# HGRN2 attention: level operands in places of their own, and the level products of a head in two groups instead of five

## The chip, the cores and the metric

The kernel runs on one core of one Trainium2 chip. The metric is the device time of one execution in microseconds, the median of several executions. A core has a matrix engine (TensorE, PE in the rows, with its weight loads as PEld), a vector engine (VectorE, DVE), a scalar engine (ScalarE, ACT), GpSimd (POOL) and a queue that issues DMAs (SyncE, SP). Each engine takes its instructions in an order that is fixed when the program is built, and they wait for each other through semaphores.

## The reference, cut to what matters

One decoder layer over 2048 tokens of width 1024: an RMS norm, one input projection, an HGRN2 group and a Mamba-2 group side by side, one output projection, a residual and a last norm. The change touches the attention inside a chunk of HGRN2 alone:

```python
q = silu(q_raw);  f = lb + (1 - lb) * sigmoid(f_raw);  k = (1 - lb) * sigmoid(-f_raw)
b = cumsum(log f) over the chunk
att[t, s] = sum over d of q[t, d] * k[s, d] * exp(b[t, d] - b[s, d])      (s <= t)
o = att @ v + (q * exp(b)) @ S;    S = exp(b_last) * S + (k * exp(b_last - b))^T @ v
```

There are 8 heads of 128 x 128. The decay between two tokens differs by channel, so it has to be multiplied into q and k before a matrix product.

## The kernel before, in words

The tokens are taken in four blocks of 512 (`tb` 0 to 3), each as 4 windows of 128. The work of a block is a list of steps: a step is one projection of 128 output columns (24 matmuls of 128x512 in a high and low split, `proj`, line 384), or one of the four steps of `v_step` (line 629). A head of HGRN2 (`hg_unit`) has three of them, `pf`, `pq`, `pg`; a pair of Mamba-2 heads (`m2_unit`) has two, `px`, `pz`. Through most of a block they alternate, H and M, five steps a pair. Each unit brings smaller pieces of work with due steps, counted from its start: after each step `flush` emits those that are due. So the small work of a head stands between the projections of the next units. Inside an engine, a scheduler in the build then sets the order.

For a head, the pieces due at steps 3 to 11 (`DUES`, line 35) are `m0, m1, m2, m3, m4, mk, m5, m6, m7`. The attention of a window is built by levels, each a product of scaled k (as weights) and scaled q (streamed):

- `m0`: the 2x2 pairs on the diagonal, product `A`: 16 matmuls with 32 weight columns and 48 streamed columns (`quarters`, line 692).
- `m1` and `m2`, both `level(b)`, with b of 2 and 8: blocks of b inside groups of 4b, products `B2` and `B8`, 16 matmuls of the same shape each. In each, VectorE first makes the scaled queries in `MB2` or `MB8`, then the products run, then VectorE scales k in place (line 756) for the next level, and picks the wanted entries of the product into `atq` with masks (line 763).
- `m3`: blocks of 32, product `H`, 8 matmuls with 32 weight columns and 32 streamed columns (line 786), after which q and k are scaled in place again (lines 792, 793) and ScalarE copies the result into `att`.
- `m4`: blocks of 64, product `G`, 4 matmuls with 64 weight columns and 64 streamed columns (line 808), then the last scaling in place (lines 814, 815).
- `mk` transposes k (`kT`), `m5` makes the state product `hS` and advances the state, `m6` makes the output `o` from `att` and the states, `m7` collects squares.

Because k and q are scaled where they stand, each level's scaling has to wait for the product of the level before it, which reads the unscaled values. Each fp32 product counts two instructions in the trace, so 16 matmuls show as x32. In the names of the rows, `A`, `B`, `H`, `G` are the banks of these products, `xn`, `S`, `yd`, `yo` those of the Mamba-2 pieces, and `csb`, `xs`, `y`, `ecs` Mamba-2 tiles. Tiles of 512 columns come from one ring of 17 places (`slot("s", ...)`), product banks from one of 6 (`bank`).

Of the kernel before, what the change touches and what calls it, by code (L numbers as in the profile page):

```python
# [7 lines left out]
F32 = mybir.dt.float32  # L8
# [3 lines left out]
ALU = mybir.AluOpType  # L12
# [4 lines left out]
P = 128  # L17
# [17 lines left out]
DUES = (3, 4, 5, 6, 7, 8, 9, 10, 11)  # L35
# [3 lines left out]
def hybrid_layer(ctx, tc, xT, wt, wdt, wout, small, out):  # L39
# [9 lines left out]
    def bank(name):  # L49
        return px.tile([P, TB], F32, tag="mx", name=name)  # L50
# [589 lines left out]
    def hg_unit(tb, hd, ws, vrec, sqs, r):  # L640
# [54 lines left out]
        def m0():
# [25 lines left out]
        def level(b):  # L721
            tot, k, atq = r["tot"], r["k"], r["atq"]
            ng = TB // (4 * b)
            gq = 32 // (4 * b)
            mb = r[f"MB{b}"]
            tt = tot.rearrange("p (g j) -> p g j", j=4)
            tb_ = lambda j, n: tt[:, :, j].unsqueeze(2).broadcast_to([P, ng, n])
            V.tensor_tensor(mb[:, :, 4, :], mb[:, :, 3, :], tb_(2, b), op=ALU.mult)
            V.tensor_tensor(mb[:, :, 5:7, :], mb[:, :, 2:5:2, :],
                            tt[:, :, 1].unsqueeze(2).unsqueeze(3).broadcast_to([P, ng, 2, b]), op=ALU.mult)  # L730
            ps = bank(f"B{b}_{nm}")
            quarters(ps, lambda Q: mb[:, Q * gq:(Q + 1) * gq, 1:7, :].rearrange("p g s r -> p g (s r)"))
            if b == 2:
                r["MB8"] = MB8 = slot("b", [16, 7, 8], f"MB8_{nm}")
                nx = MB8[:, :, 0:4, :].rearrange("p g s (j r) -> p g s j r", r=2)
                src = mb.rearrange("p (g s) j r -> p g s j r", s=4)
                t0 = tot.rearrange("p (g s j) -> p g s j", s=4, j=4)[:, :, :, 0]
                A.copy(nx[:, :, :, 0, :], src[:, :, :, 0, :])
                V.tensor_tensor(nx[:, :, :, 1, :], src[:, :, :, 1, :],
                                t0.unsqueeze(3).broadcast_to([P, 16, 4, 2]), op=ALU.mult)  # L740
                V.tensor_tensor(nx[:, :, :, 2:4, :].rearrange("p g s j r -> p g s (j r)"),
                                src[:, :, :, 5:7, :].rearrange("p g s j r -> p g s (j r)"),
                                t0.unsqueeze(3).broadcast_to([P, 16, 4, 4]), op=ALU.mult)
            else:
                r["qa"] = slot("s", [TB], f"qa{nm}")
                nx = r["qa"].rearrange("p (g j r) -> p g j r", j=4, r=8)
                A.copy(nx[:, :, 0, :], mb[:, :, 0, :])
                V.tensor_tensor(nx[:, :, 1, :], mb[:, :, 1, :], tb_(0, 8), op=ALU.mult)
                V.tensor_tensor(nx[:, :, 2:4, :].rearrange("p g j r -> p g (j r)"),
                                mb[:, :, 5:7, :].rearrange("p g j r -> p g (j r)"), tb_(0, 16), op=ALU.mult)  # L750
            V.tensor_tensor(tt[:, :, 2], tt[:, :, 2], tt[:, :, 3], op=ALU.mult)
            V.tensor_tensor(tt[:, :, 1], tt[:, :, 1], tt[:, :, 2], op=ALU.mult)
            nt = mp.tile([P, ng], F32, tag=f"tot{4 * b}", bufs=1, name=f"tot{4 * b}_{nm}")
            V.tensor_tensor(nt, tt[:, :, 0], tt[:, :, 1], op=ALU.mult)
            kv = k.rearrange("p (g j r) -> p g j r", j=4, r=b)[:, :, 0:3, :]
            V.tensor_tensor(kv, kv, tt[:, :, 1:4].unsqueeze(3).broadcast_to([P, ng, 3, b]), op=ALU.mult)  # L756
            r["tot"] = nt
            av = atq.rearrange("p w (g j r) -> p w g j r", j=4, r=b)
            pv5 = ps[:, 0:192].rearrange("p (w g s r) -> p w g s r", w=NW, s=6, r=b)
# [7 lines left out]

        def m1():
            level(2)

        def m2():
            level(8)
            r["att"] = att = atts[hd % 2]
            for j in range(4):
                qs = slice(32 * j, 32 * j + 32)
                G.tensor_copy(att[qs, :, qs], r["atq"][qs])

        def m3():

            tot, k, qa, att = r["tot"], r["k"], r["qa"], r["att"]  # L780
            ph = bank(f"H{nm}")
            ph2 = ph[:, 0:64].rearrange("p (y c) -> p y c", y=2)
            for w in range(NW):
                for i in range(2):
                    o, p0 = w * P + 64 * i, 64 * (w % 2) + 32 * i
                    T.matmul(ph2[p0:p0 + 32, w // 2, :], lhsT=k[:, o:o + 32], rhs=qa[:, o + 32:o + 64],
                             start=True, stop=True)
            t32 = tot.rearrange("p (g j) -> p g j", j=2)
            q32 = qa.rearrange("p (g j r) -> p g j r", j=2, r=32)
            k32 = k.rearrange("p (g j r) -> p g j r", j=2, r=32)  # L790
            b32 = lambda j: t32[:, :, j].unsqueeze(2).broadcast_to([P, 8, 32])
            V.tensor_tensor(q32[:, :, 1, :], q32[:, :, 1, :], b32(0), op=ALU.mult)
            V.tensor_tensor(k32[:, :, 0, :], k32[:, :, 0, :], b32(1), op=ALU.mult)
            r["t64"] = t64 = mp.tile([P, 8], F32, tag="tot64", bufs=1, name=f"tot64_{nm}")
            V.tensor_tensor(t64, t32[:, :, 0], t32[:, :, 1], op=ALU.mult)
            for a in range(2):
                for i in range(2):
                    A.copy(att[64 * i:64 * i + 32, a::2, 64 * i + 32:64 * i + 64],
                           ph2[64 * a + 32 * i:64 * a + 32 * i + 32, :, :])

        def m4():

            k, qa, att, t64 = r["k"], r["qa"], r["att"], r["t64"]
            ph = bank(f"G{nm}")
            ph2 = ph[:, 0:128].rearrange("p (y c) -> p y c", y=2)
            for w in range(NW):
                o, p0 = w * P, 64 * (w % 2)
                T.matmul(ph2[p0:p0 + 64, w // 2, :], lhsT=k[:, o:o + 64], rhs=qa[:, o + 64:o + 128],
                         start=True, stop=True)
# [50 lines left out]
        def m7():  # L860
# [16 lines left out]
        return [pf_raw, pq_raw, pg_raw] if raw else [pf, pq, pg], list(zip(DUES, (m0, m1, m2, m3, m4, mk, m5, m6, m7)))  # L877
# [336 lines left out]
```

## Time and profile before

| | us |
|---|---|
| median of 3 runs | 1907.94 (1904.02 to 1909.02) |
| the profiled execution, its own time | 1906.3 |
| its span, first to last instruction | 1904.6 |
| PE busy, share of the span | 1871.4 (98%) |
| weight loads busy | 1542.0 (81%) |
| DVE busy | 1183.6 (62%) |
| ACT busy | 707.1 (37%) |
| POOL busy | 295.7 (16%) |

The page gives the busy time of each engine first. The chain that ended last is followed back from the last instruction, and it lists what the end of the program really waited for, in order of time; two pieces of that chain that touch show no gap. A row of a timeline has the start, the time from the first start to the last end, the engine and line, the tiles written and read, and the idle time before it with what ended that.

### The profile page before, as it was taken

Reading aid. Unit: us, or ns where it says so; the run is one execution under the profiler, and the core shown is the slowest. Engines: PE = TensorE matmul, PEld = TensorE weight load, DVE = VectorE, ACT = ScalarE, POOL = GpSimd, SP = SyncE. Lnnn points to the kernel's source line nnn. Section 1 sums busy time; section 2 is a strip of 40 time slices with the busy share of each in tenths; the row PEclk is TensorE's granted clock in tenths of the full one; section 3 lists DMA queues with packets and bytes.
Section 4 is the critical chain, followed back from the end, with each engine's and each line's share of the span. In section 5 each row is a group of like instructions: output and inputs, shape, how many; then the busy total and the mean of one; then the engine's idle time right before and its main releaser. Section 6 shows DMA issues by size and latency. Waiting matters only on the chain.

```text
span 1904.6 us, 33504 instructions
## 1 busy us (share of the span) xinstructions
PE 1871.4 (98%) x13226; PEld 1542.0 (81%) x13226; DVE 1183.6 (62%) x2874; ACT 707.1 (37%) x1175; POOL 295.7 (16%) x390
## 2 busy tenths in 40 slices
PE   7899999999999999999999999999999999999998
PEld 5688887787888888878887887888888877888897
DVE  7678768955575478556664785476456764544452
ACT  4446445533352245234433533343333432211211
POOL 1432242302001211020012111201110130000000
PEclk9999999999999999999999999999999999999998
DMA  7676866754555556455555555554555375424142
GB/s 279 237 267 235 299 253 220 271 177 156 172 187 196 178 178 218 141 173 187 172 199 175 194 193 198 169 189 158 173 186 171 104 239 178 150 83 159 46 143 85
DMA packets 118316, 351.84 MB, mean 185 GB/s; under 512 B 14928, under 2 KB 26352, under 8 KB 117776
## 3 DMA queue, kind: packets, MB, share of 16 engines
q1 hardware_dynamic: 117056, 348.46, 54.4%
q8 instruction: 104, 1.70, 0.4%
q10 hardware_dynamic: 1104, 1.26, 0.2%
q14 instruction: 52, 0.43, 0.1%
HBM read 269.69 MB, written 79.97 MB: 184 GB/s over the span
## 4 chain that ended last, share of the span: by engine, by line
PE 91%; DVE 5%; DMA 2%; issue 1%; ACT 1%; POOL 0%; ACTq 0%; SPq 0%; DVEq 0%; POOLq 0%
PE po L1076 17%; PE px L384 9%; PE pz L384 9%; PE pv L629 9%; PE pf L384 9%; PE pq L384 9%; PE pg L384 8%; PE pB L384 2%; PE pC L384 2%; PE yd L578 2%; PE B L692 2%; PE o L852 1%; PE S L569 1%; PE hS L833 1%; PE yo L589 1%; PE o L851 1%
## 5 line engine op out<-in xcount | busy, mean ns | idle before, releaser
L1076 PE MATMUL po<-mh,woh 128*128 128x512 f32 (+1 forms) x640 | 224.1, 351 | 1.0 <-ACT mh L1064 1.0
L1076 PE MATMUL po<-mh,wol 128*128 128x512 f32 (+1 forms) x640 | 221.9, 347 | 0.2 <-DVE wol L1027 0.2
L1076 PE MATMUL po<-ml,woh 128*128 128x512 f32 (+1 forms) x640 | 220.1, 347 | 0.0
L1076 PEld LDWEIGHTS po<-mh,woh 128*128 128x128 f32 x640 | 121.2, 189 | 19.4 <-ACT mh L1064 2.1
L1076 PEld LDWEIGHTS po<-mh,wol 128*128 128x128 f32 x640 | 121.2, 189 | 15.7 <-issue 0.7
L1076 PEld LDWEIGHTS po<-ml,woh 128*128 128x128 f32 x640 | 120.6, 189 | 15.9 <-DVE ml L1065 0.9
L1064 ACT CAST mh<-mr 128x1024 fp32r<-128x1024 f32 (+1 forms) x41 | 36.1, 883 | 180.7 <-PE po L1076 159.0
L542 DVE TENSOR_SCALAR csb<-csb,cs 128x128 f32<-128x128 f32 x256 | 67.9, 335 | 26.9 <-ACT ecs L539 26.9
L1065 DVE TENSOR_TENSOR ml<-mr,mh 128x1024 fp32r<-128x1024 f32 (+1 forms) x39 | 39.0, 999 | 65.1 <-ACT mh L1064 65.0
L842 DVE SCALAR_TENSOR_TENSOR hSt<-hgS,totw,hS 128x128 f32<-128x128 f32 x32 | 11.0, 345 | 105.8 <-PE hS L833 102.0
L471 DVE SCALAR_TENSOR_TENSOR xs<-u_x,sm,xs 128x512 f32<-128x512 f32 x96 | 71.8, 748 | 4.7 <-ACT xs L469 4.4
L756 DVE TENSOR_TENSOR k<-k,tot 128x384 f32<-128x384 f32 x64 | 43.7, 683 | 47.2 <-PE B L692 47.2
L629 PE MATMUL pv<-wh,hh 128*128 128x512 f32 x224 | 72.0, 403 | 0.0
L468 POOL COPY hist<-u_x 128x3 f32<-128x3 f32 x32 | 9.8, 307 | 399.9 <-ACT u_x L466 399.7
L629 PE MATMUL pv<-wh,hl 128*128 128x512 f32 x224 | 69.3, 391 | 0.0
L629 PE MATMUL pv<-wl,hh 128*128 128x512 f32 x224 | 69.2, 390 | 0.0
L384 PE MATMUL px<-hh,wh 128*128 128x512 f32 x256 | 68.6, 410 | 0.0
L384 PE MATMUL pz<-hh,wh 128*128 128x512 f32 x256 | 67.5, 406 | 0.0
L466 ACT COPY u_x<-px 128x512 f32<-128x512 f32 x32 | 18.7, 585 | 129.9 <-PE px L384 129.9
L601 POOL TENSOR_TENSOR sqa<-sqa,ecs 128x512 f32<-128x512 f32 x24 | 31.6, 1318 | 222.3 <-ACT ecs L600 185.9
L384 PE MATMUL pf<-hh,wh 128*128 128x512 f32 x248 | 65.4, 406 | 0.0
L384 PE MATMUL pg<-hh,wh 128*128 128x512 f32 x248 | 65.3, 404 | 0.0
(339 smaller groups left out, 4565.8 us busy)
## 6 DMA issues: line engine op xcount, KB each, us to landing
wh<-whd SPq DMA_DIRECT2D x156, 512.0 KB, 4.3
wl<-wld SPq DMA_DIRECT2D x156, 512.0 KB, 3.4
whd<-wh SPq DMA_DIRECT2D x52, 512.0 KB, 3.6
wld<-wl SPq DMA_DIRECT2D x52, 512.0 KB, 3.7
wr<-wt SPq DMA_DIRECT2D x51, 512.0 KB, 5.1
csb<-csd SPq DMA_DIRECT2D x32, 512.0 KB, 5.5
mr<-mixd SPq DMA_DIRECT2D x50, 256.0 KB, 2.9
mixd<-sg SPq DMA_DIRECT2D x32, 256.0 KB, 2.1
```

The costliest lines, as they stand in the source:

```text
L384: state["mm"] = T.matmul(ps, lhsT=a[:, k, :], rhs=b[:, k, :], start=(n == 0), stop=(n == 23))
L471: V.scalar_tensor_tensor(dst, u[:, j:j + TB], cw[:, c, j:j + 1], dst, op0=ALU.mult, op1=ALU.add)
L542: V.tensor_scalar(csb[:, i, w, :], csb[:, i, w, :], dts["cs"][:, w, h0 + i:h0 + i + 1], 0.0, ALU.subtract, ALU.min)
L569: T.matmul(pS[:, sl], lhsT=bc["Bn"][:, w, :], rhs=xdc[:, sl], start=True, stop=True)
L578: T.matmul(pd[64 * i:64 * i + 64, w * P:(w + 1) * P], lhsT=xdt[:, w * P + i * 64:w * P + i * 64 + 64], rhs=csb[:, i, w, :], start=True, st ...
L601: G.tensor_tensor(sq["acc"], sq["acc"], t, op=ALU.add)
L629: T.matmul(ps, lhsT=a[:, 2 * j + k, w * P:(w + 1) * P], rhs=rhs, start=(j == 0 and n == 0), stop=(j == 3 and n == 5))
L692: T.matmul(ps[32 * j:32 * j + 32, 48 * w:48 * w + 48], lhsT=k[:, 32 * Q:32 * Q + 32], rhs=cols(Q), start=True, stop=True)
L756: V.tensor_tensor(kv, kv, tt[:, :, 1:4].unsqueeze(3).broadcast_to([P, ng, 3, b]), op=ALU.mult)
L1064: A.copy(mh[:, :, 0:n], mr[:, :, 0:n])
L1065: lo.tensor_tensor(ml[:, :, 0:n], mr[:, :, 0:n], mh[:, :, 0:n].bitcast(F32), op=ALU.subtract)
L1076: T.matmul(pss[d], lhsT=a[:, d, :], rhs=b, start=(first and n == 0), stop=(e == 15 and n == 2))
```

## The change

Three things are changed in `hg_unit`, and the mathematics is the same.

1. Scaled operands get places of their own. k scaled for the level of 2 is written to a new tile `k1` (one ScalarE copy for the odd tokens, one VectorE product for the even ones) and no longer over k. For the levels of 32 and 64 the scaled halves of k and q go to a new tile `hq` and to `qa` and the old place of k. So a product and the scaling for the next one do not touch the same data.
2. The products are issued in two groups. A new piece `m0b`, due at step 4, has the pairs and the blocks of 2 in one bank; `m2`, now due at step 7, has the blocks of 8, 32 and 64 in one bank. `m0` (step 3) and `m1` (step 5) have no matmul left.
3. `DUES` loses an entry, and the row of totals `totw` gets a second place.

The count of instructions on PE, SP and POOL stays as it was, 3620, 794 and 299 rows of the program's order. For a head, VectorE has 38 instructions where it had 35 (three of the scalings are split in two halves), ScalarE four short copies more.

```diff
-DUES = (3, 4, 5, 6, 7, 8, 9, 10, 11)
+DUES = (3, 4, 5, 7, 8, 9, 10, 11)
...
         def m0():
...
-            psA = bank(f"A{nm}")
-            quarters(psA, lambda Q: mvA[:, Q, :])
...
-            V.tensor_tensor(k2[:, :, 0], k2[:, :, 0], f2[:, :, 1], op=ALU.mult)
+            r["k1"] = k1 = slot("s", [TB], f"k1{nm}")
+            V.tensor_tensor(k1e[:, :, 0], ke[:, :, 0], f2[:, :, 1], op=ALU.mult)
+            A.copy(k1e[:, :, 1], ke[:, :, 1])
+            slots_of(MB2, 2, tot)
+
+        def m0b():
+            psA = bank(f"A{nm}")
+            quarters(psA[:, 0:192], k, lambda Q: mvA[:, Q, :])
+            quarters(psA[:, 192:384], k1, level_cols(MB2, 4))
...
+            level_out(psA[:, 192:384], 2)
...
         def m1():
-            level(2)
...
+            V.tensor_tensor(kv, kv, tt[:, :, 1:4].unsqueeze(3).broadcast_to([P, 64, 3, 2]), op=ALU.mult)
+            slots_of(MB8, 8, nt)
+            k4 = r["k"]
+            r["H"] = hq = slot("s", [2, 8, 32], f"hq{nm}")
+            r["qa"] = qa = slot("s", [TB], f"qa{nm}")
...
+            for i, dst in ((0, par(qa, 0)), (1, eight(hq[:, 1]))):
+                A.copy(dst[:, :, 0, :], mq[:, :, i, 0, :])
+                V.tensor_tensor(dst[:, :, 1, :], mq[:, :, i, 1, :], bq(8), op=ALU.mult)
+                V.tensor_tensor(dst[:, :, 2:4, :].rearrange("p g j r -> p g (j r)"),
+                                mq[:, :, i, 5:7, :].rearrange("p g j r -> p g (j r)"), bq(16), op=ALU.mult)
+            t32 = totals(nt, 8)
+            for i, dst in ((0, eight(hq[:, 0])), (1, par(k4, 1))):
+                V.tensor_tensor(dst[:, :, 0:3, :], par(k1, i)[:, :, 0:3, :],
+                                tq[:, :, i, 1:4].unsqueeze(3).broadcast_to([P, 8, 3, 8]), op=ALU.mult)
+                A.copy(dst[:, :, 3, :], par(k1, i)[:, :, 3, :])
...
+            V.tensor_tensor(blk(k4, 0), hq[:, 0], b32(1), op=ALU.mult)
+            V.tensor_tensor(blk(qa, 1), hq[:, 1], b32(0), op=ALU.mult)
...
         def m2():
-            level(8)
+            ps = bank(f"B{nm}")
+            quarters(ps[:, 0:192], r["k1"], level_cols(r["MB8"], 1))
...
+                    T.matmul(ph2[p0:p0 + 32, w // 2, :], lhsT=hq[:, 0, 2 * w + i, :], rhs=hq[:, 1, 2 * w + i, :],
+                             start=True, stop=True)
...
+                T.matmul(pg2[p0:p0 + 64, w // 2, :], lhsT=k4[:, o:o + 64], rhs=qa[:, o + 64:o + 128],
+                         start=True, stop=True)
+            level_out(ps[:, 0:192], 8)
...
-        def m3():
...
-        def m4():
...
-        return [...], list(zip(DUES, (m0, m1, m2, m3, m4, mk, m5, m6, m7)))
+        return [...], list(zip(DUES, (m0, m0b, m1, m2, mk, m5, m6, m7)))
```

`slots_of`, `level_out` and `totals` are the parts of the old `level(b)`: the scaled queries (lines 728 and 729), the masked copies (lines 760 to 766) and the running totals (lines 751 to 754). After the change the products of `quarters` stand at line 691, the 32 and 64 ones at 819 and 823, the last scaling of k at 833.

On PE, in the third block (`tb` 2), this is the place from the projections of head 7 to the transposes of the Mamba-2 tile. Before:

```order
L692 MATMUL B8_6_2_11127<-MB8_6_2_11054,k6_2_10770 32x48 x16
L384 MATMUL pf7_2_11174<-hh2_7073,wh151_10964 128x512 x8
L384 MATMUL pf7_2_11174<-hh2_7073,wl151_10965 128x512 x8
L384 MATMUL pf7_2_11174<-hl2_7074,wh151_10964 128x512 x8
L786 MATMUL H6_2_11203<-qa6_2_11144,k6_2_10770 32x32 x8
L384 MATMUL pq7_2_11238<-hh2_7073,wh152_11066 128x512 x8
L384 MATMUL pq7_2_11238<-hh2_7073,wl152_11067 128x512 x8
L384 MATMUL pq7_2_11238<-hl2_7074,wh152_11066 128x512 x8
L808 MATMUL G6_2_11265<-qa6_2_11144,k6_2_10770 64x64 x4
L390 MATMUL xn6_2_11276<-ident_69,xs6_2_10963 128x128 x4
```

And with the change:

```order
L384 MATMUL pf7_2_11294<-hh2_7139,wh151_11080 128x512 x8
L384 MATMUL pf7_2_11294<-hh2_7139,wl151_11081 128x512 x8
L384 MATMUL pf7_2_11294<-hl2_7140,wh151_11080 128x512 x8
L384 MATMUL pq7_2_11341<-hh2_7139,wh152_11190 128x512 x8
L384 MATMUL pq7_2_11341<-hh2_7139,wl152_11191 128x512 x8
L384 MATMUL pq7_2_11341<-hl2_7140,wh152_11190 128x512 x8
L691 MATMUL B6_2_11368<-MB8_6_2_11249,k16_2_11064 32x48 x16
L819 MATMUL B6_2_11368<-hq6_2_11260 32x32 x8
L823 MATMUL B6_2_11368<-qa6_2_11261,k6_2_10884 64x64 x4
L390 MATMUL xn6_2_11414<-ident_69,xs6_2_11079 128x128 x4
```

`B8`, `H` and `G` of head 6 stood apart, with a projection of 24 matmuls between each two; now the three stand together behind `pq`, ahead of `xn`, and nothing is left between `pf` and `pq`.

A little later on PE, from the transposes of k to the next projection `pz`. Before:

```order
L390 MATMUL kT6_2_11318<-ident_69,k6_2_10770 128x128 x4
L692 MATMUL A7_2_11326<-mvA7_2_11233,k7_2_11169 32x48 x16
L384 MATMUL px7_2_11367<-hh2_7073,wh154_11234 128x512 x8
L384 MATMUL px7_2_11367<-hh2_7073,wl154_11235 128x512 x8
L384 MATMUL px7_2_11367<-hl2_7074,wh154_11234 128x512 x8
L833 MATMUL hS6_2_11402<-v10_2_9733,kn6_2_11323 128x128 x2
L833 MATMUL hS6_2_11402<-v11_2_9734,kn6_2_11323 128x128 x2
L569 MATMUL S6_2_11411<-xdc6_2_11283,BC1_2_10115 128x128 x4
L578 MATMUL yd6_2_11423<-csb6_2_10961,xn6_2_11281 64x128 x8
L692 MATMUL B2_7_2_11436<-MB2_7_2_11343,k7_2_11169 32x48 x16
L384 MATMUL pz7_2_11469<-hh2_7073,wh155_11286 128x512 x8
```

And with the change:

```order
L390 MATMUL kT6_2_11456<-ident_69,k6_2_10884 128x128 x4
L384 MATMUL px7_2_11489<-hh2_7139,wh154_11337 128x512 x8
L384 MATMUL px7_2_11489<-hh2_7139,wl154_11338 128x512 x8
L384 MATMUL px7_2_11489<-hl2_7140,wh154_11337 128x512 x8
L856 MATMUL hS6_2_11524<-v10_2_9835,kn6_2_11461 128x128 x2
L856 MATMUL hS6_2_11524<-v11_2_9836,kn6_2_11461 128x128 x2
L569 MATMUL S6_2_11533<-xdc6_2_11421,BC1_2_10235 128x128 x4
L578 MATMUL yd6_2_11545<-csb6_2_11077,xn6_2_11419 64x128 x8
L691 MATMUL A7_2_11556<-mvA7_2_11336,k7_2_11289 32x48 x16
L691 MATMUL A7_2_11556<-MB2_7_2_11464,k17_2_11469 32x48 x16
L384 MATMUL pz7_2_11599<-hh2_7139,wh155_11424 128x512 x8
```

`A` of head 7 has left its place between `kT` and `px`, and stands with the blocks of 2 (the second row of `A7`, which reads `MB2_7` and the new tile `k17`) behind `yd`.

On DVE, the stretch behind the output product `o5` of the same block, up to the first instruction that reads the projection `pf7`. Before:

```order
L856 SCALAR_TENSOR_TENSOR sg5_2_10514<-o5_2_11098,sm_75,sg5_2_10514 128x512
L591 TENSOR_TENSOR ecs5_2_10821<-yo5_2_11112,ecs5_2_10821 128x512
L561 SCALAR_TENSOR_TENSOR m2S_198<-mS5_2_11017,ecl2_8262,S5_2_11012 128x64
L593 TENSOR_TENSOR y5_2_11033<-y5_2_11033,ecs5_2_10821 128x512
L756 TENSOR_TENSOR k6_2_10770<-k6_2_10770,tot8_6_2_11060 128x16x24
L594 TENSOR_TENSOR y5_2_11033<-y5_2_11033,sz5_2_10685 128x512
L763 COPY_PREDICATED atq6_2_10949<-mask8_515,B8_6_2_11127 128x4x24
L763 COPY_PREDICATED atq6_2_10949<-mask8_515,B8_6_2_11127 128x4x8
L763 COPY_PREDICATED atq6_2_10949<-mask8_515,B8_6_2_11127 128x4x16
L792 TENSOR_TENSOR qa6_2_11144<-qa6_2_11144,tot32_6_2_11150 128x8x32
L793 TENSOR_TENSOR k6_2_10770<-k6_2_10770,tot32_6_2_11150 128x8x32
L670 TENSOR_SCALAR f7_2_11168<-f7_2_11168,oml_190,lb_189 128x512
```

And with the change:

```order
L879 SCALAR_TENSOR_TENSOR sg5_2_10640<-o5_2_11222,sm_75,sg5_2_10640 128x512
L591 TENSOR_TENSOR ecs5_2_10918<-yo5_2_11236,ecs5_2_10918 128x512
L792 TENSOR_TENSOR hq6_2_11260<-MB8_6_2_11249,tot8_6_2_11255 128x8x8
L593 TENSOR_TENSOR y5_2_11149<-y5_2_11149,ecs5_2_10918 128x512
L793 TENSOR_TENSOR hq6_2_11260<-MB8_6_2_11249,tot8_6_2_11255 128x8x16
L594 TENSOR_TENSOR y5_2_11149<-y5_2_11149,sz5_2_10803 128x512
L797 TENSOR_TENSOR hq6_2_11260<-k16_2_11064,tot8_6_2_11255 128x8x24
L804 TENSOR_TENSOR qa6_2_11261<-hq6_2_11260,tot32_6_2_11270 128x8x32
L803 TENSOR_TENSOR k6_2_10884<-hq6_2_11260,tot32_6_2_11270 128x8x32
L670 TENSOR_SCALAR f7_2_11288<-f7_2_11288,oml_190,lb_189 128x512
```

The masked copies behind `B8` (line 763) and the two scalings behind `H` (lines 792 and 793) are gone from here, and the scalings that make `hq6`, `qa6` and `k6` for the blocks of 32 and 64 (lines 792 to 804) stand in their place, all ahead of `f7`.

## Rows read from the trace of the kernel before

**Rows 1.** The page, busy time of each engine and its share of the span.

```profile
PE 1871.4 (98%) x13226; PEld 1542.0 (81%) x13226; DVE 1183.6 (62%) x2874; ACT 707.1 (37%) x1175; POOL 295.7 (16%) x390
```

**Rows 2.** Waits of PE: line, what it waited for, us in total, times, longest.

```profile
PE B L692 <- DVE tot L751: 5.0, 1, 5.0
PE A L692 <- DVE mvA L702: 2.9, 1, 2.9
...
PE H L786 <- DVE k L756: 1.3, 1, 1.3
```

**Rows 3.** The chain that ended last, one H and M pair: start, us, what.

```profile
1427.98 0.44 PE kT L390 x4
1428.42 0.48 PE A L692 x32
1428.89 5.69 PE px L384 x24
1434.58 0.89 PE hS L833 x8
...
1436.37 1.02 PE yd L578 x16
1437.39 0.48 PE B L692 x32
...
1446.23 0.48 PE B L692 x32
1446.71 5.67 PE pf L384 x24
1452.38 0.26 PE H L786 x16
1452.64 5.66 PE pq L384 x24
1458.30 0.38 PE G L808 x8
...
1459.27 5.49 PE pg L384 x24
```

**Rows 4.** The same chain in block 0, projections with no narrow product around them.

```profile
100.11 5.47 PE pf L384 x24
105.58 5.44 PE pq L384 x24
```

**Rows 5.** Timeline of DVE in the pair of rows 3.

```profile
1444.03 0.35 DVE L842 SCALAR_TENSOR_TENSOR hgS<-hSt,totw,hS 128x128 f32<-128x128 f32 x1 [2.05 <-PE o L852]
...
1449.20 0.28 DVE L748 TENSOR_TENSOR qa<-MB,tot 128x128 f32<-128x128 f32 x1
1449.40 0.42 DVE L749 TENSOR_TENSOR qa<-MB,tot 128x256 f32<-128x256 f32 x1
...
1459.07 1.22 DVE L546 TENSOR_TENSOR csb<-csb,BC 128x1024 f32<-128x1024 f32 x1
```

**Rows 6.** The chain in head 0 of block 0, at the start.

```profile
34.73 0.69 DVE f L316
...
56.09 0.87 PE B L692 x32
56.95 4.81 PE pv L629 x11
...
67.69 0.38 PE G L808 x8
68.07 3.76 PE dt L403 x16
```

**Rows 7.** The chain in block 0, heads 6 and 7.

```profile
370.08 4.78 DVE csb L542 x8
...
379.15 0.87 PE A L692 x32
380.02 6.78 PE px L384 x24
```

**Rows 8.** Busy time by stretch: us, PE, PEld, DVE, ACT, POOL, PEclk, DMA, GB/s.

```profile
0.00:60.00 60.00, 43.23 (x246) 32.34 (x247) 48.45 (x107) 26.43 (x41) 17.47 (x21) 0.93 0.79 285
...
340.00:360.00 20.00, 20.00 (x180) 17.10 (x179) 19.97 (x44) 10.19 (x16) 8.18 (x5) 1.00 0.72 262
...
720.00:740.00 20.00, 20.00 (x180) 17.10 (x179) 19.74 (x51) 9.40 (x14) 5.30 (x4) 1.00 0.67 223
```

More of the change, by code (lines that the diff above doesn't have):

```diff
@@ L693, in quarters, with slots_of, level_cols, level_out @@
                              rhs=cols(Q), start=True, stop=True)
+        def slots_of(mb, b, tot):
+            ng = TB // (4 * b)
+            tt = tot.rearrange("p (g j) -> p g j", j=4)
+            V.tensor_tensor(mb[:, :, 4, :], mb[:, :, 3, :], tt[:, :, 2].unsqueeze(2).broadcast_to([P, ng, b]),
+                            op=ALU.mult)
+            V.tensor_tensor(mb[:, :, 5:7, :], mb[:, :, 2:5:2, :],
+                            tt[:, :, 1].unsqueeze(2).unsqueeze(3).broadcast_to([P, ng, 2, b]), op=ALU.mult)
+        def level_cols(mb, gq):
+            return lambda Q: mb[:, Q * gq:(Q + 1) * gq, 1:7, :].rearrange("p g s r -> p g (s r)")
+        def level_out(ps, b):
+            gq = 32 // (4 * b)
+            av = r["atq"].rearrange("p w (g j r) -> p w g j r", j=4, r=b)
+            pv5 = ps.rearrange("p (w g s r) -> p w g s r", w=NW, s=6, r=b)
+            for s0, s1, j0 in ((0, 3, 1), (3, 4, 3), (4, 6, 2)):
+                n = s1 - s0
+                mkk = masks[b][:, :, s0:s1, :].rearrange("p g s r -> p g (s r)")
+                V.copy_predicated(
+                    av[:, :, :, j0:j0 + n, :].rearrange("p w g s r -> p w g (s r)"),
+                    mkk.unsqueeze(1).broadcast_to([P, NW, gq, n * b]),
+                    pv5[:, :, :, s0:s1, :].rearrange("p w g s r -> p w g (s r)"))
+        def totals(tot, b):
+            tt = tot.rearrange("p (g j) -> p g j", j=4)
+            V.tensor_tensor(tt[:, :, 2], tt[:, :, 2], tt[:, :, 3], op=ALU.mult)
+            V.tensor_tensor(tt[:, :, 1], tt[:, :, 1], tt[:, :, 2], op=ALU.mult)
+            nt = mp.tile([P, TB // (4 * b)], F32, tag=f"tot{4 * b}", bufs=1, name=f"tot{4 * b}_{nm}")
+            V.tensor_tensor(nt, tt[:, :, 0], tt[:, :, 1], op=ALU.mult)
+            return nt
         def m0():
@@ L719, in m0 @@
                               maskPi.unsqueeze(1).broadcast_to([P, NW, 16]), pA[:, :, 32:48])
[L721 to L725, printed above, removed]
-            tt = tot.rearrange("p (g j) -> p g j", j=4)
[L727 to L759, printed above, removed]
-            for s0, s1, j0 in ((0, 3, 1), (3, 4, 3), (4, 6, 2)):
-                n = s1 - s0
-                mkk = masks[b][:, :, s0:s1, :].rearrange("p g s r -> p g (s r)")
-                V.copy_predicated(
-                    av[:, :, :, j0:j0 + n, :].rearrange("p w g s r -> p w g (s r)"),
-                    mkk.unsqueeze(1).broadcast_to([P, NW, gq, n * b]),
-                    pv5[:, :, :, s0:s1, :].rearrange("p w g s r -> p w g (s r)"))
@@ L774, in m2 @@
+            for w in range(NW):
+                o, p0 = w * P, 64 * (w % 2)
+                T.matmul(pg2[p0:p0 + 64, w // 2, :], lhsT=k4[:, o:o + 64], rhs=qa[:, o + 64:o + 128],
+                         start=True, stop=True)
+            level_out(ps[:, 0:192], 8)
             for j in range(4):
@@ L776, in m2 @@
                 G.tensor_copy(att[qs, :, qs], r["atq"][qs])
-        def m3():
[L780 to L799, printed above, removed]
-        def m4():
[L803 to L809, printed above, removed]
             t64v = t64.rearrange("p (g j) -> p g j", j=2)
             q64 = qa.rearrange("p (g j r) -> p g j r", j=2, r=64)
-            k64 = k.rearrange("p (g j r) -> p g j r", j=2, r=64)
+            k64 = k4.rearrange("p (g j r) -> p g j r", j=2, r=64)
             b64 = lambda j: t64v[:, :, j].unsqueeze(2).broadcast_to([P, NW, 64])
@@ L815, in m4 @@
             V.tensor_tensor(q64[:, :, 1, :], q64[:, :, 1, :], b64(0), op=ALU.mult)
-            r["tw"] = tw = mp.tile([P, NW], F32, tag="totw", bufs=1, name=f"totw_{nm}")
+            r["tw"] = tw = mp.tile([P, NW], F32, tag="totw", bufs=2, name=f"totw_{nm}")
             V.tensor_tensor(tw, t64v[:, :, 0], t64v[:, :, 1], op=ALU.mult)
             for a in range(2):
-                A.copy(att[0:64, a::2, 64:128], ph2[64 * a:64 * a + 64, :, :])
+                for i in range(2):
+                    p0 = 64 * i
+                    A.copy(att[p0:p0 + 32, a::2, p0 + 32:p0 + 64], ph2[64 * a + 32 * i:64 * a + 32 * i + 32, :, :])
+            for a in range(2):
+                A.copy(att[0:64, a::2, 64:128], pg2[64 * a:64 * a + 64, :, :])
         def mk():
@@ L876, in m7 @@
             nc.sync.dma_start(fold, rc)
[L877 removed]
+        return [pf_raw, pq_raw, pg_raw] if raw else [pf, pq, pg], list(zip(DUES, (m0, m0b, m1, m2, mk, m5, m6, m7)))
     pend = []
```

44 lines of the change are left out of this document (37 added, 7 removed).

## The prediction

> **What bounds the kernel now.** I read the busy shares first: PE works 98% of the span, DVE 62%, ACT 37%, POOL 16% [rows 1]. The list of PE's waits comes next, since a wait per head would show there as 32 waits of one kind. It shows three single ones at the pieces the change touches, 5.0, 2.9 and 1.3 us, and none that recurs [rows 2]. So in the steady part PE always has something to do, and only what PE itself takes, or a new wait, can move the end.
>
> The chain of waits then shows what PE's time is made of. In the pair of steps that I use as the pattern its pieces touch end to start. The reader should compare equal projections there, 24 matmuls each: behind a group of narrow products they take 5.69 (`px`, behind `A`), 5.67 (`pf`, behind `B8`) and 5.66 us (`pq`, behind `H`), and 5.49 (`pg`) behind transposes of full width [rows 3]. Where no narrow product stands around, `pf` takes 5.47 and `pq` 5.44 [rows 4]. A narrow group therefore costs PE not only its own row, but 0.2 us in the projection behind it.
>
> The small groups have a fixed part too. `hS` streams 8 records of 128 columns in 0.89 us, 0.87 ns a column. An instruction of a fp32 product counts two records, and a product with 32 weight columns seems to run four side by side: `A` would take 32 x 48 x 0.87 / 4 = 0.33 us and takes 0.48; `H` 16 x 32 x 0.87 / 4 = 0.11 and takes 0.26; `G`, two side by side, 8 x 64 x 0.87 / 2 = 0.22 and takes 0.38; `yd`, 64 weight columns, 0.89 and takes 1.02 [rows 3]. About 0.15 us stays each time, whatever the size. That four run side by side is my reading, an estimate that makes all four rows agree.
>
> **The change, part by part.**
>
> *Groups that join, on PE.* A head has five groups (`A`, `B2`, `B8`, `H`, `G`), and will have two. No product goes away, so only edges can be saved:
> - `A` leaves the place ahead of `px`, which then stands behind `kT`, of full width: 5.69 - 5.49 = 0.20 us.
> - `B8` leaves the place ahead of `pf`: 5.67 - 5.47 = 0.20 us.
> - `H` leaves the place ahead of `pq`: 5.66 - 5.44 = 0.22 us.
> - `pz` keeps a narrow group ahead of it, the joint one, and `xn` still stands behind `G`: nothing.
> - `A` and `B2` stand together: one fixed part less, 0.15 us. `B8` and `H` likewise: 0.15 us.
> - `H` to `G` goes from 32 to 64 weight columns. Bounds: 0 if that costs as much as an edge to a wide product, 0.15 if it is free. I take 0, by the nearest row: `yd` with 64 columns, between wide products, still carries 0.13 [rows 3].
>
> That is 0.92 us a head, and 32 heads make 29.4 us. Low bound: only the three projections, 0.62 x 32 = 19.8; high bound 1.07 x 32 = 34.2.
>
> The Trainium skill, page "TensorEngine Tiling (Array Packing)", section "Key Properties", says that changing the tiling mode, but not just the tile, drains TensorE. By that rule the 29.4 would stand, since `H` to `G` changes the mode; without it the gain would be 34.2. No row here has a 64-column group directly behind a 32-column one.
>
> *The start, head 0 of block 0.* Here PE waits 5.0 us ahead of `B8` [rows 2], and the 11 `pv` records behind take 4.81 us [rows 6], where 11 x 5.47 / 24 = 2.5 is the price elsewhere [rows 4]; the mean granted clock of the first 60 us is 0.93 [rows 8], so I read the slow records as a fallen clock after the idle time. With the change all four v steps stand ahead of the joint group. They would end at 68.07 - 5.0 - 2.3 - 0.87 - 0.26 - 0.38 = 59.3. DVE begins at 34.73 [rows 6] and needs, by my count of its rows up to the last scaling for `G`, about 27 us, so it is ready at about 61.7; the group ends at about 62.7 where it ended at 68.07. That is 5.3 us less; the same wait, now 2.4 us, may again cost clock, up to the 2.7 us that it cost. I take -4 us, bounds -1 and -7.
>
> *Heads 6 and 7 of block 0.* DVE is full there, 19.97 of 20 us [rows 8], and PE waits for it at `H` (1.3) and `A` (2.9) [rows 2], with a slow `px` of 6.78 behind [rows 7]. These 5.3 us (1.3 + 2.9 + 1.1) would go, as both products come a step later. But the last scaling of k, which `kT` reads, now stands behind the product that finishes `csb` on DVE, and that waits for ACT; with `csb` at 4.78 us here [rows 7], `kT` may wait about as long. What is late next is `kT`. I take 0, bounds -5 and +5.
>
> *VectorE.* Three instructions more for each head, scalings split into halves. Bounds from rows of the shapes: 128x128 takes 0.28, 128x256 0.42 [rows 5], both with a start cost in them, so a split adds 0.1 to 0.15, together 0.2 to 0.45 us a head, 7 to 14 us in all. I cost it at nothing: PE covers it. In the pattern pair the state update `hgS` starts at 1444.03, and the last scaled query of the old level stands at 1449.40 [rows 5]; the new scalings take the place of the three masked copies, `L792` and `L793`, so they end near 1450.5. PE reaches the joint group at 1446.23 + 5.47 + 5.44 = 1457.1 [rows 3, 4]. Cover: near 7 us. For `kT` the last scaling comes behind `csb`, at 1459.07 + 1.22 + 0.4 = 1460.7 [rows 5], and `kT` is due behind `pg`, at about 1464: cover 3 us. If the cover is gone, each us goes to the end.
>
> *ScalarE.* Four short copies a head, about 1 us, on an engine at 37% [rows 1]; they are inside the same cover. They have one thing behind them: the scalings of DVE that read their halves.
>
> *Places and banks.* Two more tiles a head come from the ring of 17; `hq` often gets the place of the head before's `qa`, which its output product `o` reads last, so its first write waits for `o`; `hgS` at 1444.03 waits for that same `o` [rows 5], so this is in the cover above. Banks: two a head for five. SP and POOL issue the same rows in the same order of steps, no DMA is added: nothing.
>
> **The sum.** 1906.3 - 29.4 - 4 + 0 = 1872.9 us for an execution like the profiled one; the median of the runs is 1.6 above that one, so 1874.
>
> **The rivals.**
>
> *DVE late in the full stretches.* DVE has 19.97 and 19.74 us of 20 in two stretches of blocks 0 and 1 [rows 8], with no slack to take 0.45 us more a head and a chain of longer scalings. For: PE waits there today [rows 2]. Against: in the second one PE has its full 20.00. Price: heads 5 to 7 of three blocks, 9 heads at 1 to 2 us, so 1883 to 1892, say 1885. It decides once DVE is over 7 us behind PE. Chance 0.13.
>
> *The edges move along.* If the 0.2 and 0.15 us belong to the small products themselves (each loads new weights before so few columns), joining saves nothing, and only the start gains: 1907.9 - 4 = 1904. For: weight loads are 1542.0 us busy [rows 1], and no row shows two narrow groups together. Against: the 0.2 us stands in the projection, not in the group. The Trainium skill, "TensorE: Matmul & The Clock Gate", Part 3 (packing), has weight loads overlap running matmuls only when their row groups differ; all tiles here take all 128 rows, so by that rule this rival would be the case. Chance 0.05.
>
> *Slower: PE waits in each head at the joint group.* The three levels now need all their scalings before the first product: `o` frees `hq`, ACT does `on` and then the copies, DVE the six scalings, and only then may PE begin, with the next projections queued behind. Today each level waited for its own part only. Break-even is at (29.4 + 4) / 32 = 1.04 us of wait a head. At 2 us a head the time is 1874 + 64 = 1938, at 3 us 1970. It decides where DVE and ACT need over 13 us behind `o` instead of the 6 to 7 counted above. For: DVE is full in places [rows 8]. Against: 7 us of cover in the pattern. Chance 0.07.
>
> **How the numbers follow.** The forecast gets 0.75. Its own bounds are 1874 - 3 - 5 - 4.8 = 1861 and 1874 + 3 + 5 + 9.6 = 1892; not all fall together, so 1863 to 1893 holds it and most of the first rival, and leaves out the two others. About 0.3%, 5.7 us, is what a measurement tells from no change. The forecast and the first rival are faster by more (0.88), the second nearly all the same (0.04, with 0.01 faster for a larger gain at the start), the third slower: 0.89, 0.04, 0.07.
>
> **What would show it.** Right: `px` behind `kT` near 5.49, `pf` and `pq` near 5.45; `A` with `B2` as one piece of near 0.8, `B8`, `H`, `G` as one of 0.8 to 0.97; no wait of PE that recurs; the end of the start section (`dt`) near 63. Wrong: `px` or `pf` still at 5.66 (second rival); a line of waits with many counts at the joint `B` (third), or at `kT` for DVE (first, and the bound of heads 6 and 7).

## The result and the profile after

| | before | after |
|---|---|---|
| median | 1907.0 us (1904.02 to 1909.02, 4 runs) | 1882.72 us (1881.20 to 1884.37, 4 runs) |
| ratio, 95% interval | | 0.9874 (0.9857 to 0.9891) |
| profiled execution: own time, span | 1906.3, 1904.6 | 1884.4, 1882.7 |

The change takes 24.3 us off the median, 1.3%, where 33 were forecast. The two profiled executions are 21.9 us apart. The first line of the page, which answers to [rows 1]:

```profile
PE 1849.1 (98%) x13226; PEld 1539.6 (82%) x13226; DVE 1196.7 (64%) x2970; ACT 732.2 (39%) x1303; POOL 315.0 (17%) x390
```

PE has the same count of instructions and is 22.3 us less busy, about what the span lost: the gain was in the time that the same products take. DVE has 13 us more, ACT 25.

The chain of waits for the pair that answers to [rows 3] (start, us, what):

```profile
1404.96 0.44 PE kT L390 x4
1405.40 5.49 PE px L384 x24
...
1413.69 0.82 PE A L691 x64
1414.51 5.67 PE pz L384 x24
...
1422.86 5.49 PE pf L384 x24
1428.35 5.44 PE pq L384 x24
1433.79 0.48 PE B L691 x32
1434.27 0.12 PE B L819 x16
1434.39 0.38 PE B L823 x8
1434.77 0.59 PE xn L390 x4
...
1440.87 0.44 PE kT L390 x4
```

From one `kT` to the next the pair takes 1440.87 - 1404.96 = 35.91 us, where it took 1464.76 - 1427.98 = 36.78 (the second `kT` of the kernel before stands in the rows below). `px` lost 0.20 us, `pf` 0.18, `pq` 0.22. `A` with `B2` takes 0.82 for twice 0.48. In the joint group the blocks of 8 still take 0.48, being first, but the blocks of 32 take 0.12 where they took 0.26, and `G` keeps its 0.38. `pz` pays as before. Each term of the forecast can be read off one row.

PE's waits, which answer to [rows 2] (line, what it waited for, us in total, times, longest):

```profile
PE kT L390 <- DVE k L833: 4.6, 1, 4.6
PE B L819 <- DVE hq L797: 2.8, 1, 2.8
PE dt L403 <- ACT v L635: 2.4, 1, 2.4
...
PE yo L589 <- DVE hgS L865: 1.4, 1, 1.4
```

At the pieces that the change touches no wait recurs: one per place, at the start (`B`, `dt`), in block 0 (`kT`) and at the end of block 3 (`yo`). To see what each stretch gave, the same `kT` is followed through the chains, first before, then after: heads 0 and 7 of block 0, then of block 3 (before: the end of the pair of [rows 3] and head 6; after: head 6), and the long row of the output projection.

```profile
71.83 0.44 PE kT L390 x4
...
416.97 0.44 PE kT L390 x4
...
1464.76 0.44 PE kT L390 x4
1501.54 0.44 PE kT L390 x4
...
1636.28 87.06 PE po L1076 x384
```

```profile
71.92 0.44 PE kT L390 x4
...
411.70 0.44 PE kT L390 x4
...
1476.77 0.44 PE kT L390 x4
...
1613.15 87.06 PE po L1099 x384
```

| stretch | forecast | after minus before |
|---|---|---|
| to the first `kT` | -4 | +0.09 |
| first `kT` to that of head 7, block 0 | 7 heads, and 0 for the waits | -5.36 |
| from there to head 6 of block 3 | 23 heads | -19.50 |
| from there into the output projection (87.06 us row) | a head | +1.64 |
| from there to the end | 0 | +1.23 |

The 23 undisturbed heads give 0.85 us each. At that rate the 7 heads ahead should have given 5.93, so the full stretch of block 0 lost 0.57 net. The last line differs from execution to execution: for the sum of squares at the end the chain shows 32 records in 4.2 to 4.7 us in four profiles (this one, `b8_apart`, `all_apart`, `best`), and only 16 of them, in 1.70 us, in the ten others. The instructions are the same: on the timeline all 32 take 4.85 us here and 3.63 in the kernel before. I put it down to none of the edits.

### The profile page after: what moved, and what is told of

Same layout as the page of the kernel before. It is cut to its first block, busy times and chain, and to the rows that moved or that the text cites. A ratio compares the mean times of both kernels' runs of the same rounds, so it can differ in the third digit from the quotient of the medians.

```text
span 1882.7 us, 33875 instructions
## 1 busy us (share of the span) xinstructions
PE 1849.1 (98%) x13226; PEld 1539.6 (82%) x13226; DVE 1196.7 (64%) x2970; ACT 732.2 (39%) x1303; POOL 315.0 (17%) x390
## 4 chain that ended last, share of the span: by engine, by line
PE 91%; DVE 5%; DMA 2%; issue 1%; ACT 1%; POOL 0%; DVEq 0%; SPq 0%; POOLq 0%; ACTq 0%
PE po L1099 17%; PE pz L384 9%; PE px L384 9%; PE pf L384 9%; PE pg L384 9%; PE pq L384 8%; PE pv L629 8%; PE pB L384 2%; PE pC L384 2%; PE yd L578 2%; PE yo L589 1%; PE hS L856 1%; PE S L569 1%; PE o L875 1%; PE o L874 1%; PE A L691 1%
## 5 line engine op out<-in xcount | busy, mean ns | idle before, releaser
L828 POOL COPY att<-atq 32x128 f32<-32x128 f32 x128 | 63.3, 495 | 260.1 <-DVE atq L713 256.1
L128 POOL TENSOR_TENSOR wl<-wr,wh 128x1024 fp32r<-128x1024 f32 x21 | 54.0, 2569 | 64.6 <-ACT wh L127 64.6
L384 PE MATMUL pq<-hh,wh 128*128 128x512 f32 x248 | 64.7, 401 | 0.0
```

The source lines that it names most:

```text
L128: (G if i == 2 or c >= 32 else V).tensor_tensor(lo, raw, hi.bitcast(F32), op=ALU.subtract)
L384: state["mm"] = T.matmul(ps, lhsT=a[:, k, :], rhs=b[:, k, :], start=(n == 0), stop=(n == 23))
```

## The experiments

All are edits of the changed kernel, and their times are to be held against its 1882.7. "Edge theory" in the expectations is the forecast's reading: the price belongs to the place where narrow and wide groups meet. The diffs are cut to what matters; `...` marks what is left out.

**One join undone, and the other.** `B8` gets a bank and a piece of its own (`m1b`, due at step 6); in the second run `A` does (`m0a`, due at step 3).

```diff
-DUES = (3, 4, 5, 7, 8, 9, 10, 11)
+DUES = (3, 4, 5, 6, 7, 8, 9, 10, 11)
...
-        return ..., list(zip(DUES, (m0, m0b, m1, m2, mk, m5, m6, m7)))
+        return ..., list(zip(DUES, (m0, m0b, m1, m1b, m2, mk, m5, m6, m7)))
```

```diff
-DUES = (3, 4, 5, 7, 8, 9, 10, 11)
+DUES = (3, 3, 4, 5, 7, 8, 9, 10, 11)
...
-        return ..., list(zip(DUES, (m0, m0b, m1, m2, mk, m5, m6, m7)))
+        return ..., list(zip(DUES, (m0, m0a, m0b, m1, m2, mk, m5, m6, m7)))
```

> The changed kernel with one join undone: the products of the blocks of 8 stand alone again, between pf and pq, in a bank of their own; the places of the operands stay as in the changed kernel. Edge theory: pq goes from 5.44 back to about 5.66 us, and the group of 16 products gets its own fixed part of about 0.15 us (the three together 0.98 now, 0.48 and 0.64 or so apart), 0.37 us a head, 32 heads: 1882.7 + 11.8 = 1894.5, between 1891 and 1898. Rival (the gain comes from the operands' own places, which take waits between DVE and PE away, and grouping is worth nothing): 1882.7 within 3 us, pq at 5.44.

> The changed kernel with the other join undone: the products of the pairs stand alone again behind kT, ahead of px; the blocks of 2 stay where they are. Edge theory: px goes from 5.49 back to about 5.69 us, A and B2 apart take 0.96 for 0.82, together 0.34 us a head: 1882.7 + 10.9 = 1893.6; up to 4 us more if PE waits for mvA in the full stretch of block 0, so 1891 to 1898. Rival (places, not grouping): 1882.7 within 3 us.

Measured: 1892.06 us (ratio to before 0.9914, 0.9893 to 0.9934) and 1894.35 us (0.9928, 0.9911 to 0.9945). The chain of the first, and of the second:

```profile
1435.99 0.48 PE B L691 x32
1436.47 5.66 PE pq L384 x24
1442.13 0.26 PE B L823 x16
```

```profile
1415.84 0.48 PE A L691 x32
1416.32 5.67 PE px L384 x24
```

Putting the group of 16 products ahead of `pq` makes `pq` 0.22 us longer and gives the blocks of 32, which come first in their group again, their 0.14 us back (0.26), although nothing of their operands changed. In the second run `px` is 0.18 us longer, and `A` and `B2` take 0.48 each again. Both runs came where the edge theory put them, and both exclude the rival.

**All groups apart, the new places kept.** `H` and `G` are split as well, with their old steps 6 and 7, and `B8` is due at 5; the order on PE is the old one.

```diff
-DUES = (3, 4, 5, 7, 8, 9, 10, 11)
+DUES = (3, 3, 4, 5, 5, 6, 7, 8, 9, 10, 11)
...
-        return ..., list(zip(DUES, (m0, m0b, m1, m2, mk, m5, m6, m7)))
+        return ..., list(zip(DUES, (m0, m0a, m0b, m1, m1b, m2a, m2, mk, m5, m6, m7)))
```

> The operands keep the new places of the change, but all five groups of products stand apart again, in the order of the kernel before (B8 ahead of pf, H ahead of pq, G ahead of xn, A ahead of px, B2 ahead of pz). Edge theory: the steady pair takes 36.8 us again, for 35.9, over 30 intervals of heads 26 us: 1882.7 + 26 = 1909, between 1904 and 1912, so the places alone are worth nothing in time. Rival (the places, which let the scalings run ahead of the products, bring part of the gain): 1890 to 1900.

Measured: 1906.92 us, ratio 0.9994 (0.9983 to 1.0005): no difference from the kernel before. Its pair takes 36.76 us again (from the `kT` at 1426.61 in the chain). The places alone are worth nothing in time. They are what permits the joins, since a product no longer has to be done before the next scaling.

**G with 32 weight columns.**

```diff
-                T.matmul(pg2[p0:p0 + 64, w // 2, :], lhsT=k4[:, o:o + 64], rhs=qa[:, o + 64:o + 128],
...
+                for h in (0, 32):
+                    T.matmul(pg2[p0 + h:p0 + h + 32, w // 2, :], lhsT=k4[:, o + h:o + h + 32], rhs=qa[:, o + 64:o + 128],
...
```

> The changed kernel with G as 8 products of 32 weight columns where it has 4 of 64, the same entries. If the 0.15 us that G carries is the price of going from 32 to 64 weight columns, its row falls from 0.38 to about 0.23 us, and xn behind stays at 0.58 or rises to 0.64: 0.09 to 0.15 us a head, 1878 to 1880. Rival (each group of products has the fixed part on its own, whatever its width): the row stays at 0.38 or grows with twice the instructions, 1883 to 1888.

Measured: 1879.82 us (0.9854, 0.9839 to 0.9869). `G` in the chain:

```profile
1429.70 0.25 PE B L824 x16
```

Twice the instructions, and the row falls from 0.38 to 0.25 us. So what `G` carried was the step from 32 to 64 columns, and not a price of each group. The Trainium skill, "TensorEngine Tiling (Array Packing)", section "Key Properties", says that a change of the tiling mode drains TensorE and a change of tile alone does not; the trace agrees as far as this change has a price, 0.13 us; that a drain is what takes it no row shows.

**yd with 32 columns too.** 16 products of 32 columns for 8 of 64, with `G` as in the run above.

```diff
-                for i in range(2):
-                    T.matmul(pd[64 * i:64 * i + 64, w * P:(w + 1) * P],
-                             lhsT=xdt[:, w * P + i * 64:w * P + i * 64 + 64], rhs=csb[:, i, w, :],
+                for c4 in range(4):
+                    T.matmul(pd[32 * c4:32 * c4 + 32, w * P:(w + 1) * P],
+                             lhsT=xdt[:, w * P + c4 * 32:w * P + c4 * 32 + 32], rhs=csb[:, c4 // 2, w, :],
...
```

> The changed kernel with both groups of 64 weight columns made of 32 columns: G (as in g32, 0.13 us a head) and yd (16 products of 32 columns for 8 of 64), so that yd, A and B2 form one stretch of 32-column products. Edge theory: yd and the group behind it share one fixed part of 0.13 to 0.15 us, so yd with A and B2 take about 1.70 for 1.84: 0.13 + 0.13 = 0.26 us a head, 8.3 in all, 1882.7 - 8.3 = 1874.4, between 1872 and 1878. Rival (a product has its own price, and twice as many of yd cost more): 1879.8 or slower.

Measured: 1876.10 us (0.9840, 0.9822 to 0.9858), the fastest of all kernels here: 6.6 us less than the change, 31 less than before.

```profile
1441.76 1.01 PE yd L578 x32
1442.77 0.69 PE A L691 x64
```

`yd` takes the same with twice the records, and the group behind it loses its fixed part, 0.69 for 0.82.

**All narrow work of a pair in one place.** As above, and the joint group two steps later, behind `yd`; `kT`, `hS` and `o` of the head follow it.

```diff
-MDUES = (3, 4, 6, 7)
-M0DUES = (4, 5, 7, 8)
+MDUES = (3, 4, 5.75, 7)
+M0DUES = (4, 5, 6.75, 8)
-DUES = (3, 4, 5, 7, 8, 9, 10, 11)
+DUES = (3, 4, 5, 9, 10, 11, 12, 13)
```

> As narrow, and the joint group B8, H, G of a head two steps later, behind the yd of its pair and ahead of the A and B2 of the next head, with all that follows for the head two steps later too: one narrow stretch for a pair of steps. Edge theory: one fixed part (0.15) and the slower piece behind (xn 0.59 for 0.44) go, 0.29 us a head, 9.3 in all: 1874.4 - 9.3 = 1865. Rival (k, hq, qa and sg hold their places of the ring for two steps more, so that writers wait for readers, and the work of the last head reaches two steps further into the output projection): 1870 to 1885, with waits of PE for DVE or ACT that recur.

Measured: 1903.06 us (0.9980, 0.9968 to 0.9992). The forecast of the edge held and the time did not. Chain of a pair in block 3, then PE's waits:

```profile
1416.84 0.34 PE B L691 x32
...
1417.55 0.68 PE A L691 x64
...
1438.90 0.44 PE xn L390 x4
```

```profile
PE dt L403 <- ACT v L635: 7.2, 1, 7.2
PE A L691 <- issue: 6.9, 4, 3.1
PE po L1100 <- ACT woh L1050: 4.8, 1, 4.8
```

`B8` behind `yd` takes 0.34 us instead of 0.48, `xn` 0.44 instead of 0.59, and the pair 35.33 us (from `xn` at 1403.57 to the next). But PE now waits at many places, 18.9 us in these three rows alone. The 7.2 at `dt` are no loss: they stand for 5.6 us in three waits at that place in `narrow`, and the first `pz` starts 1.0 us earlier. By the starts of `pz` the profiled execution is 9.3 us behind that of `narrow` at the end of block 0 and 9.8 at the end of block 3, where 24 heads at 0.34 should have brought it 8 us forward, and 24.0 at the end of the program. That is 10 us lost in block 0, the gain of blocks 1 to 3 used up there, and 14 lost behind the last `pz`. The same was then tried in blocks 1 and 2 alone (`DUES` and `MDUES` chosen by `tb`), and once more with the new tile of the run `knew` below.

> As narrow, with the joint group two steps later, behind yd, in the second and third block alone, where merge_all took 35.33 us for a steady pair (35.68 in narrow) and PE had no wait; first and last block as in narrow. Edge theory: 16 heads x 0.35 = 5.6 us less than narrow, 1876.1 - 5.6 = 1870.5. Rival (the waits that made merge_all slow belong to the later group everywhere, not to the full stretches of the first and last block): 1876 to 1888.

> As narrow_m12, with the k for the state in a tile of its own as in knew, which was 1 to 3 us below the changed kernel: 1868 to 1870. If the place that it takes from the ring of 17 for longer is one too many where the group stands later: 1872 to 1880, with waits of DVE or ACT for readers.

Measured: 1883.13 us (0.9868, 0.9851 to 0.9886) and 1891.08 us (0.9909, 0.9892 to 0.9926): slower than `narrow` by 7 and 15 us (5 and 13 by the ratios, each to the kernel before as timed beside it). In the trace of `narrow_m12`, which is of an execution 4.9 us faster than its median, blocks 1 and 2 take 3.1 us more than in `narrow`, where 5.6 less were expected. The waits are not of the full stretches of the first and last block alone. What makes them is open: the largest new one in each of the three kernels is at `A` (6.9, 4.2 and 8.6 us), and the trace names no releaser for it ("issue").

**The ring.** One place less for the changed kernel.

```diff
-NS = 17
+NS = 16
```

> The changed kernel with 16 places in the ring of 512-column tiles where it has 17; the order of the work is not touched otherwise. If the two more tiles of a head (k1 and hq) still leave the ring with a place to spare, as the prediction has it: 1882.7 within 3 us and the steady pair at 35.9 us. Rival (the ring is at its limit, which would also be why the later group of merge_all and narrow_m12 costs waits): writers on DVE or ACT wait for the last reader of a place, PE's waits for DVE rise, 1887 to 1900.

Measured: 1882.03 us (0.9868, 0.9852 to 0.9885), and the pair takes 35.90 us. The two new tiles of a head leave a place to spare. Whether the kernels with the later group lack places was not tried.

**More work on VectorE.**

```diff
-            V.tensor_tensor(blk(k4, 0), hq[:, 0], b32(1), op=ALU.mult)
+            for _ in range(7):
+                V.tensor_tensor(blk(k4, 0), hq[:, 0], b32(1), op=ALU.mult)
```

> The changed kernel with one scaling ahead of the joint group (128x256 on DVE) done seven times over with the same result: 6 x 0.34 = 2.0 us more on DVE for each head, between the product before and the joint group. If the cover of 7 us is there, the steady pair stays at 35.9 us and only the start and the full stretch of block 0 pay, 2 us for three or four heads: 1889 to 1893. Rival (PE waits for DVE at the joint group in each head, the slower case of the prediction): up to 2 us x 32 = 64, 1947.

Measured: 1898.39 us (0.9958, 0.9942 to 0.9973), 15.7 more; the range was missed by 5. The chain, and the longest of the new waits:

```profile
1412.26 0.44 PE kT L390 x4
...
1448.17 0.44 PE kT L390 x4
```

```profile
PE B L824 <- DVE k L804: 9.0, 4, 5.0
```

The steady pair stays at 35.91 us: 2 us more per head are hidden there to the last hundredth. The first `kT` is 3.6 us later than in the changed kernel (75.48), and head 7 of block 0 is 7.25 later (418.95); from there the distance does not grow until 1412, and the rest comes at the end of block 3, which the expectation had left out.

**The start: the joint group behind dt.** `DUES` of the very first head with 8 for 7, and 9 to 12 behind.

> The changed kernel with the joint group of the very first head, and what follows for that head, one step later, so that the products of dt stand ahead of it. If the waits of PE at that group and at dt (2.8, 0.5 and 2.4 us) and the slow dt behind (6.39 us for 3.76) come from the order of these two: up to 8.3 us less, 1875 to 1879. Rival (DVE and ACT reach the eviction of v, which frees the bank for dt, no sooner; the wait is the same under another name): 1881 to 1884.

Measured: 1882.05 us (0.9872, 0.9855 to 0.9890): no change. Chain from the last scaling to `dt`, start, us, what:

```profile
63.10 0.34 DVE qa L805
...
64.60 0.67 DVE x L363
...
65.91 0.60 ACT v L636
66.64 5.42 PE dt L404 x16
```

`dt` needs what stands at the end of a queue on DVE (`x`, from which `hh` is cast on ACT, and then the eviction of `v` behind that cast). Whether the group stands ahead of `dt` or behind, `dt` starts when DVE is through.

**The wait at kT.** The scaled k for the state gets a tile of its own, made ahead of the joint group.

```diff
+            r["kz"] = kz = slot("s", [TB], f"kz{nm}")
...
+            V.tensor_tensor(kz64[:, :, 0, :], k64[:, :, 0, :], t64b, op=ALU.mult)
+            A.copy(kz64[:, :, 1, :], k64[:, :, 1, :])
...
-            transpose4(pk, r["k"])
+            transpose4(pk, r["kz"])
```

> The changed kernel with k scaled for the state written to a new tile, ahead of the joint group on DVE, so that kT no longer waits for a scaling that stands behind csb. If the 4.6 us of waiting at kT in block 0 and the slow kT and px behind it (1.12 for 0.44, 7.64 for 5.49) hang on that one instruction: 1882.7 - 4.6 - 0.7 - 2.1 = 1875. Rival (DVE is full there, so that the next reader of its data waits instead, A for mvA or hS for kn, or the one more place taken from the ring makes a writer wait): 1879 to 1886. Elsewhere no change, since no other kT waits.

Measured: 1881.25 us (0.9862, 0.9847 to 0.9876), 1.5 less, the rival's value. Waits, and the chain of block 0:

```profile
PE px L384 <- DVE atq L713: 3.6, 1, 3.6
```

```profile
362.47 4.86 DVE csb L542 x8
...
369.77 0.61 ACT mvA L678
370.40 0.69 DVE mvA L679
371.24 7.31 PE px L384 x24
```

The wait at `kT` is gone and `px` waits instead. `csb` on DVE, the load of ACT's next function, `mvA` on ACT and its product on DVE come ahead of `px`; I read that as its bank, which `pq` holds until `mvA` is read. The same chain ended at `A` in the kernel before [rows 7], so the change gave this wait another name.

## Why the prediction was right, and where it was off

The median, 1882.7, lies nearer to the first rival's 1885 than to the forecast's 1874, so the number alone does not tell the two apart; the rows do. The gain is at the edges, and of the first rival's waits little came in.

- **The edges, 0.92 us a head: right, at 0.87.** Every term stood: 0.20, 0.18, 0.22 in the projections (0.20, 0.20, 0.22 forecast), 0.14 and 0.14 for the joins (0.15 each), 0 for `H` to `G`. The runs with a join undone gave each back, and `all_apart` the whole. The rival that edges move along with the products is excluded. Two readings of the forecast were wrong here and did no harm: it has `yd` between wide products, and no row with two narrow groups together. In [rows 3] `B2`, 32 columns wide, follows `yd`, 64 wide, directly and keeps its whole 0.48; there the price of a change of width was to be seen, and it bears out the 0 for `H` to `G`. The Trainium skill's rule that spoke for the rival ("TensorE: Matmul & The Clock Gate", Part 3: weight loads overlap running products only when the row groups differ) does not hold for these column tiles: in `merge_all` 32 records of 48 columns, with 32 loads over all 128 rows, take 0.34 us, which is 32 x 48 x 0.87 / 4 = 0.33, so the loads lie under the products. [rows 1] spoke against it before: 1871.4 us of products and 1542.0 of loads fit into a span of 1904.6, and the full-width projections, which have most of them, load all 128 rows each time.
- **32 heads: two too many.** Between the first `kT` and that of head 6 of block 3 lie 30 heads. The first head stands among the v steps and the last runs into the output projection, where neighbours differ. Heads that begin a block gave 0.74 (48.20 to 47.46 us from the `kT` of head 0 to that of head 1, blocks 1 to 3), so the mean is 0.85.
- **The start, -4: wrong, +0.09 by the first `kT`, outside its bounds of -1 and -7.** The step that failed is "the group ends at about 62.7 where it ended at 68.07. That is 5.3 us less". The count of 27 us on DVE was good (the last scaling ended near 62.3 in the changed kernel), and so was the end of the group (63.2), but I let `dt` follow the group at once. `dt` waits for work that stands behind those scalings on DVE and ACT, started at 65.53 and took 6.39 us at a low clock:

```profile
63.49 0.67 DVE x L362
...
65.53 6.39 PE dt L403 x16
```

  The granted clock from 60 to 80 us was 0.74; from 62 to 68, behind PE's waits of 2.8, 0.5 and 2.4 us, it was 0.50, the lower of its two levels (1.2 and 2.4 GHz). `dt` had taken 3.76 us in [rows 6], at 1.00 (68 to 72 us). I gave back 2.7 us for clock at most and chose less than half of it; 2.6 came on `dt` alone.
- **Heads 6 and 7 of block 0, 0 with bounds of 5: right, +0.6.** The forecast named `kT` as late next, near 5 us; it waited 4.6.

```profile
371.16 1.22 DVE csb L546
372.56 0.34 DVE k L833
372.94 1.13 PE kT L390 x4
374.07 7.64 PE px L384 x24
```

  The k scaling stands directly behind `csb`, as told from the order. `px` is slower than in [rows 7]: 7.64 for 6.78, after a wait of 4.6 us for one of 2.9.
- **VectorE and ScalarE cost nothing: right in the steady part, 1.6 us off at the end of block 3.** The cover of near 7 us was real. In the pair shown above the last scaling ahead of the joint group starts at 1426.76 and ends at 1427.18, and PE reaches the group at 1433.79, 6.6 us later:

```profile
1426.76 0.42 DVE L803 TENSOR_TENSOR k<-hq,tot 128x256 f32<-128x256 f32 x1
```

  `dve6` takes 2 us of this without effect; more was not tried. I had looked for full stretches in blocks 0 and 1 and passed over the last one, where DVE also makes the weights and inputs of the output projection. There 1.6 us were lost, the kind of loss that the first rival names, of its 9 to 18. The wait of 1.4 us at `yo` is there and was not in the kernel before: the chain has the weights `wol` (1.21 us) on DVE right ahead of `hgS`, for which `yo` waits. Up to that `yo` 1.0 of the 1.6 us is lost; the rest comes behind it, amid transfers, and its cause is not shown.
- **The slower rival: excluded.** No wait recurred at the joint group.

Together, against the profiled executions: forecast 33.4 us less, measured 21.9. Of the 11.5 us between, 4.1 are the start (0.7 of it is `pg`, which began at 26.64 for 25.96, ahead of everything that changed), 0.9 the first head, counted but without an edge to save, 2.2 the edges (30 x 0.072), 0.6 the waits in block 0, 2.6 the last head (0.9 counted, 1.6 lost) and 1.2 the end of this execution (11.6 with the roundings).

## What to carry to other kernels

On a busy matrix engine, look at the same full-size product behind different neighbours: here 5.44 to 5.49 us behind wide work and 5.66 to 5.69 behind narrow work is a price of the edge, and it went when narrow groups stood together; one width for all of them gave a little more, even with twice the instructions. A step that only moves a wait gains nothing until the last thing that the next product needs has been followed through every queue. What a later place for a group saved at its edges, 0.34 us a head, was small here beside the waits that it brought, so the order has to be tried, not only counted.

## What the runs showed that was not expected

- Four products of 32 columns really run side by side to within 0.03 us of the estimate: 0.34 us for 32 records of 48 columns behind narrow work (0.33), 0.12 for 16 of 32 (0.11), 0.25 for 16 of 64 (0.22). The first group behind wide work paid 0.14 more at both sizes that were measured so (0.48 and 0.26).
- The edge out of a narrow group costs by what follows: 0.2 us on a projection of 24 matmuls, 0.15 on four transposes (`xn` 0.59 for 0.44), and for `xn` it is the same behind 64 columns and, in `g32`, behind 32.
- After one wait of 4.6 us the next `kT` took 1.13 us for 0.44 and `px` 7.64 for 5.49, with a granted clock of 0.83 from 360 to 380: 2.8 us on top of the wait.
- POOL's copies of `att`, same count and shape, took 495 ns each for 343, and all its work 315.0 us for 295.7. No wait that the trace names hangs on these copies, and why they are slower is open.
